# Experts in two passes, with the next feed-forward run on each finished quarter of the width

## The chip, the core and the metric

The kernel runs on one core of a Trainium2 chip. TensorE (PE) multiplies matrices into PSUM, VectorE (DVE) and ScalarE (ACT) do elementwise work, GpSimd (POOL) hardly anything here, SyncE (SP) issues the transfers from device memory. What counts is the device time of one execution in microseconds; before the change it was 1604.07 (median of three, 1603.33 to 1605.59).

## The reference, cut to what matters

Two models stand one behind the other on 256 positions of width 1024. The first block ends with a mixture of 16 experts of which each takes its 32 best positions; the second block (two layers) begins with a feed-forward of width 2816.

```python
# end of the first block
aff = softmax(h @ w_router)                      # h = rms_norm(x)
gate, idx = top_k(aff.T, 32)                     # per expert
xin = h[idx]                                     # (16, 32, 1024)
hid = silu(xin @ w_gate) * (xin @ w_up)          # per expert, 1024 x 1024 each
y = (hid @ w_down) * gate
x = x + zeros.at[idx].add(y)
# start of the second block, layer 0
h = x + 0.5 * (silu(n(x) @ w_gate) * (n(x) @ w_up)) @ w_down   # n = rms_norm, 1024 -> 2816 -> 1024
# then a mixer, a second feed-forward, and the same again for layer 1
```

## The kernel before

Activations are held transposed, 128 channels by 256 positions, eight chunks `xt[:, c]`. All weights come once from device memory as one stream of 1 MB tiles (128 x 2048 words): `add` lists them in order, `fetch` (L308) issues the transfer of the next, `pump` (L316) issues as many as there are slots. A slot is one of 4 "raw" ones or, for expert weights, also one of the 17 of the ring, from which `st["hold"]` keeps some back. The ring also holds activations and the split weights.

The weights of the dense layers are cut into a high and a low part (`split`, `cut`, L325 to L342): ACT writes the high part, DVE the rest, two halves per tile, both into ring slots. A product is then the high part with both parts of the input and the low part with the input's high part. `mm3` (L417) does it as three matmuls of 256 columns into one sum, `mm2` (L422) as one of 512 columns and one of 256, whose two halves are added on the way out of PSUM. One block below is one such product of 128 x 128 weights with 256 positions. Expert weights are used as they are.

Experts (L1200 to L1268), for each of 16 in turn: 8 tiles of gate and up (`gu`, four matmuls per tile in four column groups of the array), Silu and product (`sg`, `hid`), a transposition (`tr`, `hidT`), then 4 tiles of down, one per 256 columns of the width (`y`), each followed by a copy (`ys`) and two matmuls with the matrix `scat` that add the expert's 32 rows at their positions into `macc` (`moe`). The sums of all 16 experts stay in four PSUM banks, and are complete only with the last expert. `keep_warm` puts matmuls without use (`junk`) where PE waits.

The feed-forward (`ffn`, L1273) has 22 gate and up tiles, each one unit of 128 hidden channels (16 blocks), and 11 down tiles. For the first one `first_phase` (L554) starts on the chunks as the last scatters finish. PSUM's eight banks are two pools of four (`pa` and `pb`; `pc` is `pb`), which change roles after each feed-forward (`st["turn"]`).

The order on each engine is set by a scheduler that works with costs of its own and the priorities in the code; `later` and `behind` put something back or in order. So the order of the code isn't that of an engine.

## Time and profile before

| | us |
|---|---|
| median of three runs | 1604.07 |
| the profiled execution | 1605.56 |
| its span, first to last instruction | 1603.8 |
| PE busy in the span | 1478.1 (92%) |
| DVE busy | 892.7 (56%) |
| ACT busy | 666.0 (42%) |
| bytes moved | 400.66 MB, 250 GB/s on the mean |

Matmuls are pipelined and their ends are modelled, so busy PE time says when PE had work and not how fast it went; the distance from start to start says that. The granted clock is a share of 2.4 GHz: 1.00 is that level, 0.50 is 1.2 GHz, and a figure between is a mean over both. A matmul in plain 32-bit floats has two records in the trace, so eight records of `gu` are the four matmuls of one tile.

### The profile page before, as it was taken

The numbers are of one execution on the slowest core, as the hardware profiler recorded it, in microseconds if no ns is written. First come the engines' busy times: TensorE is split into PE (matmuls) and PEld (weight loads), VectorE is DVE, ScalarE is ACT, GpSimd is POOL, SyncE is SP. The second block draws the span as 40 slices with busy tenths as digits, with TensorE's granted clock in tenths as the row PEclk, the third lists the DMA queues.
The fourth block names the chain that finished last, engine by engine and source line by source line (L and its number), as shares of the span: only waits on it lengthen the run. The fifth ranks groups of instructions, "written<-read, shape, count | busy, mean of one in ns | idle before, by whom it ended". The sixth has DMA issues, their size and how long they took to land.

```text
span 1603.8 us, 24974 instructions
## 1 busy us (share of the span) xinstructions
PE 1478.1 (92%) x10328; PEld 1146.4 (71%) x10328; DVE 892.7 (56%) x1680; ACT 666.0 (42%) x1168; POOL 6.1 (0%) x11
## 2 busy tenths in 40 slices
PE   9899988766777768999999999999999999999997
PEld 8887743322223224888889998888888899988886
DVE  7875512100000000977767977766876749877673
ACT  6445211000000000665545665555655546666462
POOL 0000000000000000000000000000000000000000
PEclk9999999877877788999999999999999999999999
DMA  7536799999999999665462545645463643635540
GB/s 295 194 104 226 292 378 420 421 421 421 420 422 421 421 421 410 223 233 207 163 218 94 211 164 192 221 164 210 163 231 135 238 146 126 252 135 211 183 158 27
DMA packets 59153, 400.66 MB, mean 250 GB/s; under 512 B 6560, under 2 KB 9760, under 8 KB 11424
## 3 DMA queue, kind: packets, MB, share of 16 engines
q1 hardware_dynamic: 58896, 398.93, 65.1%
q8 instruction: 81, 1.33, 0.3%
q14 instruction: 32, 0.26, 0.0%
q10 hardware_dynamic: 144, 0.14, 0.0%
HBM read 397.99 MB, written 1.05 MB: 249 GB/s over the span
## 4 chain that ended last, share of the span: by engine, by line
PE 69%; DMA 23%; DVE 5%; ACT 3%; issue 1%; DVEq 0%; SPq 0%; ACTq 0%
DMA w<-in_we 22%; PE gu L425 20%; PE gu L426 10%; PE dn L425 10%; PE dn L426 5%; PE acc L419 1%; PE gu L1217 1%; PE acc L418 1%; PE acc L420 1%; PE y L1260 1%; DVE wl L342 1%; ACT wh L341 1%; PE moe L1245 1%; PE junk L377 1%; PE qk L420 1%
## 5 line engine op out<-in xcount | busy, mean ns | idle before, releaser
L425 PE MATMUL gu<-xs,wh 128*128 128x512 f32 x1408 | 494.7, 395 | 0.0
L342 DVE TENSOR_TENSOR wl<-w,wh 128x1024 fp32r<-128x1024 f32 (+1 forms) x365 | 436.0, 1217 | 39.1 <-ACT wh L341 29.3
L426 PE MATMUL gu<-xs,wl 128*128 128x256 f32 x1408 | 392.0, 279 | 0.0
L341 ACT ACTIVATE wh<-w 128x1024 fp32r<-128x1024 f32 (+1 forms) x365 | 364.0, 1047 | 37.1 <-PE dn L425 20.5
L425 PEld LDWEIGHTS gu<-xs,wh 128*128 128x128 f32 x1408 | 263.7, 188 | 60.7
L426 PEld LDWEIGHTS gu<-xs,wl 128*128 128x128 f32 x1408 | 265.3, 188 | 0.5
L425 PE MATMUL dn<-hx,wh 128*128 128x512 f32 x704 | 248.5, 394 | 0.0
L426 PE MATMUL dn<-hx,wl 128*128 128x256 f32 x704 | 196.2, 279 | 0.0
L1217 PE MATMUL gu<-w,xin 128*32 128x512 f32 x1024 | 139.9, 651 | 45.3 <-DMA w<-in_we 43.9
L425 PEld LDWEIGHTS dn<-hx,wh 128*128 128x128 f32 x704 | 132.0, 187 | 30.8
L426 PEld LDWEIGHTS dn<-hx,wl 128*128 128x128 f32 x704 | 132.6, 188 | 0.0
L1245 PE MATMUL moe<-scat,ys 128*128 128x256 f32 x256 | 92.0, 495 | 28.4 <-DVE ys L1267 15.7
L1267 DVE COPY ys<-y 128x256 f32<-128x256 f32 x34 | 14.4, 424 | 186.4 <-PE y L1260 186.3
L1217 PEld LDWEIGHTS gu<-w,xin 128*32 128x32 f32 x1024 | 26.6, 112 | 127.5 <-DMA w<-in_we 87.9
L1287 ACT ACTIVATE fl<-gu 128x256 f32<-128x256 f32 x176 | 65.9, 377 | 122.5 <-PE gu L426 122.1
L1288 DVE TENSOR_TENSOR fz<-gu,fl 128x256 f32<-128x256 f32 x176 | 73.8, 420 | 71.7 <-ACT fl L1287 71.3
L1233 ACT ACTIVATE sg<-gu 64x512 f32<-64x512 f32 x16 | 9.5, 591 | 249.0 <-PE gu L1217 249.0
L1245 PEld LDWEIGHTS moe<-scat,ys 128*128 128x128 f32 x256 | 54.5, 236 | 73.5 <-DVE ys L1267 33.2
L1234 DVE TENSOR_TENSOR hid<-sg,gu 64x512 f32<-64x512 f32 x16 | 11.0, 690 | 157.0 <-ACT sg L1233 157.0
L1260 PE MATMUL y<-w,hidT 128*32 128x256 f32 x1024 | 91.2, 482 | 7.7 <-ACT hidT L1240 7.7
L1260 PEld LDWEIGHTS y<-w,hidT 128*32 128x32 f32 x1024 | 32.3, 128 | 51.0 <-issue 32.2
L1290 ACT ACTIVATE fs<-fz 128x256 f32<-128x256 f32 x88 | 36.5, 415 | 72.7 <-DVE fz L1289 72.3
(381 smaller groups left out, 2034.2 us busy)
## 6 DMA issues: line engine op xcount, KB each, us to landing
w<-in_we SPq DMA_DIRECT2D x192, 1024.0 KB, 19.8
w<-in_ffn1gu SPq DMA_DIRECT2D x44, 1024.0 KB, 5.0
w<-in_ffn2gu SPq DMA_DIRECT2D x44, 1024.0 KB, 4.9
w<-in_ffn1d SPq DMA_DIRECT2D x22, 1024.0 KB, 5.0
w<-in_wm SPq DMA_DIRECT2D x22, 1024.0 KB, 4.9
w<-in_ffn2d SPq DMA_DIRECT2D x22, 1024.0 KB, 5.0
w<-in_w SPq DMA_DIRECT2D x14, 1024.0 KB, 5.5
w<-in_wo SPq DMA_DIRECT2D x8, 1024.0 KB, 5.0
```

Source lines behind the costliest of these rows:

```text
L341: hi = S.activation(wh, raw[i][:, a0:a1], AF.Copy)
L342: lo = V.tensor_tensor(wl, raw[i][:, a0:a1], wh.bitcast(F32), op=OP.subtract)
L377: PE.matmul(junk[:, :128], lhsT=w, rhs=x, start=True, stop=True)
L420: PE.matmul(ps, lhsT=wh, rhs=x[:, 1], start=False, stop=last, skip_group_check=True)
L425: PE.matmul(ps, lhsT=wh, rhs=x, start=first, stop=False, skip_group_check=True)
L426: PE.matmul(ps[:, 0], lhsT=wl, rhs=x[:, 1], start=False, stop=last, skip_group_check=True)
L1217: PE.matmul(pg[32 * g:32 * g + 32], lhsT=xin[k // 4][:, k % 4, 32 * e:32 * e + 32], rhs=w[:, g], start=k == 0, stop=k == 7, skip_group_che ...
L1245: PE.matmul(macc[s][:, m], lhsT=ys[s][:, 128 * m:128 * m + 128], rhs=sc, start=e == 0 and m == 0, stop=e == NE - 1 and m == 1, skip_group_ ...
L1260: PE.matmul(p[32 * g:32 * g + 32], lhsT=hT[:, g, k // 4], rhs=w[:, k], start=k < 4, stop=k >= 4, skip_group_check=True, tile_position=(0, ...
L1287: S.activation(zl[:, m], p[m][:, 0], AF.Copy)
L1288: V.tensor_tensor(z[:, m], p[m][:, 1], zl[:, m], op=OP.add)
L1290: S.activation(s, z[:, 0], AF.Silu)
```

## The change

The stream and the order of the experts change, and the first feed-forward of layer 0 gets code of its own.

- All 16 experts' gate and up come first (128 tiles). Their hidden values stay in two ring slots (`HT`), the positions' matrices of four experts each in `SC`.
- Down is stored anew: by quarter of the width, then by group of four experts (4 x 4 x 4 tiles). The four matmuls that run side by side in the array's column groups now belong to four experts, a group's sums stand below one another in one bank, and one pair of scatter matmuls serves all four.
- When a quarter (256 channels, two chunks) is complete (`x`), it is added to the residual, multiplied by the norm's weights and split. In the next quarter's 16 tiles the 22 units of the feed-forward's gate and up are computed on these two chunks (`u`): four blocks each, by `mm3`. The partial sums go to six ring slots (`Pt`): copied by ACT for the first quarter, added by DVE for the next ones. Their weights (`f0g`, `f0h`) are stored by quarter, 5.5 MB each, and stand between the down tiles in the stream.
- 5 units of the third quarter (`KEEP`) are kept until after the last down tile. The last quarter of the units runs with `down`, which now covers the full width at once, by `mm3` into four banks; root and Silu come only then.
- The extra `keep_warm` calls in the last expert and `first_phase` go. PSUM's second pool is 3 banks, and `pc` has one of its own.

```diff
@@ -32,7 +32,8 @@
...
 RING, RAW, T1, T2 = 17, 4, 10, 10
-WARM = (12, 32, 8, 3)
+WARM = (12, 32)
+KEEP, EARLY = 5, 2
 ATTN = (1, 1, 1, 1, 2)
...
@@ -158,13 +159,21 @@
...
     g, u = f["w_expert_gate"][0], f["w_expert_up"][0]
     gu = np.concatenate([g.reshape(NE, 8, 128, 1024), u.reshape(NE, 8, 128, 1024)], axis=3)
-    dn = f["w_expert_down"][0].reshape(NE, 8, 128, 4, 256).transpose(0, 3, 2, 1, 4).reshape(NE, 4, 128, 2048)
-    out["we"] = np.concatenate([gu, dn], axis=1)
+    out["we"] = gu
+    dn = f["w_expert_down"][0].reshape(4, 4, 4, 2, 128, 4, 256)
+    out["wd"] = dn.transpose(5, 0, 2, 4, 3, 1, 6).reshape(4, 4, 4, 128, 2048)
...
-        return psum.tile(list(shape), F32, name=name, tag="AB"[st["turn"]], bufs=4)
+        return psum.tile(list(shape), F32, name=name, tag="A", bufs=4)
     def pb(name, shape=(128, 2, 256)):
-        return psum.tile(list(shape), F32, name=name, tag="BA"[st["turn"]], bufs=4)
+        return psum.tile(list(shape), F32, name=name, tag="B", bufs=3)
     def pc(name, shape=(128, 512)):
-        return pb(name, shape)
+        return psum.tile(list(shape), F32, name=name, tag="C", bufs=1)
+    def bank_sets():
+        n = iter(range(1 << 30))
+        def other(name, shape=(128, 2, 256)):
+            return (pb, pb, pb, pc)[next(n) % 4](name, shape)
+        return (other, pa) if st["turn"] else (pa, other)
...
-    WE = [add(a["we"][e], 12, 0) for e in range(NE - 1)]
+    WE = [add(a["we"][e], 8, 0) for e in range(NE)]
...
-    WE.append(add(a["we"][NE - 1], 11, 0))
-    first_gu = add(a["ffn1gu0"], 1, 1)
...
-    def add_ffn(n, l, *gu):
-        gu, dn = list(gu), []
-        for j in range(len(gu), NF):
+    def quarters():
+        for q in range(4):
+            yield from (("y", 0, q, i) for i in range(4))
+            yield ("sc", 0, q)
+        yield ("x", 0)
+        for s in range(1, 4):
+            n, todo = 0, 22 if s < 3 else 22 - KEEP
+            sc = None
+            for k in range(16):
+                yield ("y", s, k // 4, k % 4)
+                while n < todo and n * 13 < (k - 2) * todo:
+                    yield ("u", s - 1, n)
+                    n += 1
+                if sc:
+                    yield sc
+                sc = ("sc", s, k // 4) if k % 4 == 3 else None
+            while n < todo:
+                yield ("u", s - 1, n)
+                n += 1
+            yield sc
+            yield ("x", s)
+        yield from (("u", 2, j) for j in range(22 - KEEP, 22))
+    order, DS, GS = [], {}, {}
+    for op in quarters():
+        if op[0] == "y":
+            order.append(op[1:])
+        elif op[0] == "u" and op[2] % 4 == 0:
+            order.insert(len(order) - EARLY, ("gs", op[1], op[2] // 4))
+    for o in order:
+        if o[0] == "gs":
+            GS[o[1:]], = add([a["f0g"][o[1], o[2]] if o[2] < 5 else a["f0h"][o[1]]], 1, 1)
+        else:
+            DS[o], = add([a["wd"][o]], 1, 0)
+    d0 = []
+    for j in range(22):
...
-    macc = [pa(f"moe{b}") for b in range(4)]
...
-        sd = work.tile([128, 2, 4, 32], F32, name="sgr", tag="t1", bufs=T1)
-        for t in range(2):
-            V.tensor_scalar(sd[:, t], onehot[t][:, e].bitcast(F32)[:, None, :].to_broadcast([128, 4, 32]),
-                            aff[:, t, e:e + 1], None, op0=OP.mult)
-        pt = pc("tr")
-        for t in range(2):
-            PE.transpose(pt[:, 256 + 128 * t:384 + 128 * t], sd[:, t].rearrange("p g s -> p (g s)"), ident)
-        sc = t1("scat")
-        V.tensor_copy(sc, pt[:, 256:512])
         sg = work.tile([64, 512], F32, name="sg", tag="t2", bufs=T2)
         hid = work.tile([64, 512], F32, name="hid", tag="t2", bufs=T2)
         S.activation(sg, pg[0:64], AF.Silu)
...
-        hT = work.tile([128, 4, 2, 32], F32, name="hidT", tag="t1", bufs=T1)
-        S.activation(hT.rearrange("p j h s -> p (j h s)"), pt[:, 0:256], AF.Copy)
-        py, ys = [pb("y0", (128, 512)), pb("y1", (128, 512))], {}
-        def scatter(s):
+        if e % 8 == 0:
+            HT.append(ralloc([128, 8, 2, 4, 32], F32, "hidT"))
+            st["hold"] -= 1
+        S.activation(HT[e // 8][:, e % 8].rearrange("p h j s -> p j h s"),
+                     pt[:, 0:256].rearrange("p (j h s) -> p j h s", j=4, h=2), AF.Copy)
+        if e % 4 == 3:
+            q = e // 4
+            ps = pa("trs")
+            for t in range(2):
+                sd = work.tile([128, 4, 32], F32, name="sgr", tag="t1", bufs=T1)
+                V.tensor_tensor(sd, onehot[t][:, 4 * q:4 * q + 4].bitcast(F32),
+                                aff[:, t, 4 * q:4 * q + 4, None].to_broadcast([128, 4, 32]), op=OP.mult)
+                PE.transpose(ps[:, 0, 128 * t:128 * t + 128], sd.rearrange("p g s -> p (g s)"), ident)
+            if q % 2 == 0:
+                SC.append(t2("scat"))
+            V.tensor_copy(SC[q // 2][:, q % 2], ps[:, 0])
...
+    def quarter_steps():
+        norm, Pt, py, ys, macc = None, [], {}, {}, {}
+        def unit(s, j):
+            i = GS[s, j // 4]
+            n = 4 if j < 20 else 2
+            ahead(i)
+            wh, wl = (w[:, :512 * n].rearrange("p (c j m o) -> p c j m o", c=2, j=n, m=2) for w in parts[i])
+            p = pb("gu")
             for m in range(2):
-                PE.matmul(macc[s][:, m], lhsT=ys[s][:, 128 * m:128 * m + 128], rhs=sc,
-                          start=e == 0 and m == 0, stop=e == NE - 1 and m == 1, skip_group_check=True)
-        for s in range(4):
-            pump()
-            if e == NE - 1 and s == 3:
-                f = GU["ffn1", 0]
-                norm, ps0 = Norm(vc("ffn1n", 0, 8)), [pb("gu"), pb("gu")]
-                front = first_phase(norm, adder(macc), f[0], ps0, lambda c: c == 5 and split(f[1]))
...
-            p = py[s // 2][:, 256 * (s % 2):256 * (s % 2) + 256]
-            for k in range(8):
-                g = k % 4
-                PE.matmul(p[32 * g:32 * g + 32], lhsT=hT[:, g, k // 4], rhs=w[:, k],
-                          start=k < 4, stop=k >= 4, skip_group_check=True, tile_position=(0, 32 * g))
...
-            ys[s] = t1("ys")
-            if s % 2 or e == NE - 1:
-                st["ys"] = V.tensor_copy(ys[s], p)
+                for c in range(2):
+                    mm3(p[:, m], wh[:, c, j % 4, m], wl[:, c, j % 4, m], norm.x[2 * s + c], m == 0 and c == 0,
+                        m == 1 and c == 1)
+            if j % 4 == n - 1:
+                done(i)
+            return p
+        for op in quarters():
+            if op[0] == "y":
+                _, s, q, i = op
+                pump()
+                if i == 0:
+                    py[s, q] = pa("y", (128, 256))
+                k = DS[s, q, i]
+                w = raw[k].rearrange("p (k g n) -> p k g n", k=2, g=4)
+                for c in range(2):
+                    for g in range(4):
+                        e = 4 * q + g
+                        h = HT[e // 8][:, e % 8].rearrange("p h j s -> p (h j) s")
+                        PE.matmul(py[s, q][32 * g:32 * g + 32], lhsT=h[:, 2 * i + c], rhs=w[:, c, g],
+                                  start=i == 0 and c == 0, stop=i == 3 and c == 1, skip_group_check=True,
+                                  tile_position=(0, 32 * g))
+                done(k)
+                if i == 3:
+                    ys[s, q] = t1("ys")
+                    S.activation(ys[s, q], py.pop((s, q)), AF.Copy)
+            elif op[0] == "sc":
+                _, s, q = op
+                if q == 0:
+                    macc[s] = pa("moe")
+                y = ys.pop((s, q))
+                for m in range(2):
+                    PE.matmul(macc[s][:, m], lhsT=y[:, 128 * m:128 * m + 128], rhs=SC[q // 2][:, q % 2],
+                              start=q == 0 and m == 0, stop=q == 3 and m == 1, skip_group_check=True)
+            elif op[0] == "x":
+                s = op[1]
+                if norm is None:
+                    norm = Norm(vc("ffn1n", 0, 8))
+                for m in range(2):
+                    c = 2 * s + m
+                    V.tensor_tensor(xt[:, c], macc[s][:, m], xt[:, c], op=OP.add)
+                    norm.split(c)
+                for m in range(2):
+                    norm.square(2 * s + m)
+                if s == 0:
+                    st["hold"], st["la"], st["late"] = 7, 1, 0
+                if s == 3:
+                    rfree(2)
             else:
-                S.activation(ys[s], p, AF.Copy)
-            scatter(s)
-            if e == NE - 1 and s == 3:
-                next(front)
-    rfree(2)
...
+                _, s, j = op
+                p = unit(s, j)
+                if s == 0:
+                    if j % 4 == 0:
+                        Pt.append(ralloc([128, 4, 2, 256], F32, "Pt"))
+                        st["hold"] -= 1
+                    S.activation(Pt[j // 4][:, j % 4], p, AF.Copy)
+                else:
+                    V.tensor_tensor(Pt[j // 4][:, j % 4], p, Pt[j // 4][:, j % 4], op=OP.add)
+        return norm, Pt, unit
...
+    def first_ffn():
+        st["hold"] = 5
+        norm, Pt, unit = quarter_steps()
+        warm(AF.Silu)
+        st["hold"], st["la"], st["late"] = 1, LA[0], LATE[0]
+        ps, hs, acc = {}, {}, []
+        def evac(j):
+            z = Pt[j // 4][:, j % 4]
+            V.tensor_tensor(z, ps.pop(j), z, op=OP.add)
+            V.tensor_tensor(z, z, norm.rb2, op=OP.mult)
+            s, h = t1("fs"), t1("fh")
+            S.activation(s, z[:, 0], AF.Silu)
+            V.tensor_tensor(h, s, z[:, 1], op=OP.mult)
+            hs[j] = t2("hx", F32R)
+            hilo(hs[j][:, 1], hs[j][:, 0], h)
+        def down(j):
+            if j == 0:
+                acc.extend(pa(f"dn{b}") for b in range(4))
+            i = d0[j // 2]
+            ahead(i)
+            wh, wl = (w.rearrange("p (m o j) -> p m o j", m=2, j=128) for w in parts[i])
+            for o in range(8):
+                mm3(acc[o // 2][:, o % 2], wh[:, j % 2, o], wl[:, j % 2, o], hs[j], j == 0 and o % 2 == 0,
+                    j == NF - 1 and o % 2 == 1)
+            if j % 2:
+                done(i)
+        for j in range(3):
+            ps[j] = unit(3, j)
+            if j == 0:
+                norm.fin1(pa)
+        norm.fin2()
+        for j in range(3):
+            evac(j)
+        for j in range(3, NF):
+            ps[j] = unit(3, j)
+            evac(j)
+            down(j - 3)
+        norm.free()
+        st["hold"], st["la"], st["late"] = 2, LA[1], LATE[1]
+        for j in range(NF - 3, NF):
+            down(j)
+        rfree(6)
+        return adder(acc, 0.5)
+    def ffn(update, n, l, g):
+        P, Q = bank_sets()
         gu, dn = GU[n, l], DN[n, l]
...
```

What stands where is told by the order of each engine's instructions.

PE at an expert, kernel before. In the names, `w183` to `w187` are tiles of the stream, `hidT` the expert's hidden values.

```order
L1217 MATMUL gu_4044<-w182_3924,xin1_2369 32x512 x4
L1217 MATMUL gu_4044<-w183_3930,xin1_2369 32x512 x4
L1238 MATMUL tr_4094<-cst_86,hid_4100 128x64 x4
L1260 MATMUL y0_4109<-w184_3936,hidT_4107 32x256 x8
L1245 MATMUL moe0_2324<-scat_4097,ys_4121 128x256 x2
L1260 MATMUL y0_4109<-w185_3942,hidT_4107 32x256 x8
L1245 MATMUL moe1_2325<-scat_4097,ys_4135 128x256 x2
L1260 MATMUL y1_4110<-w186_3948,hidT_4107 32x256 x8
L1245 MATMUL moe2_2326<-scat_4097,ys_4149 128x256 x2
L1260 MATMUL y1_4110<-w187_3954,hidT_4107 32x256 x8
L1245 MATMUL moe3_2327<-scat_4097,ys_4163 128x256 x2
```

PE in the fourth quarter's down, kernel after. `w216` to `w220` are down tiles of four experts each, `gu` the units of the third quarter, `xs` the normed input.

```order
L1296 MATMUL y_4750<-w216_4690,hidT_2423 32x256 x8
L1296 MATMUL y_4750<-w217_4700,hidT_2423 32x256 x8
L1309 MATMUL moe_4773<-scat_2653,ys_4854 128x256 x2
L1296 MATMUL y_4872<-w219_4720,hidT_2957 32x256 x8
L1296 MATMUL y_4872<-w220_4798,hidT_2957 32x256 x5
L479 MATMUL gu_4818<-xs_3551,wl214_4811 128x256
L480 MATMUL gu_4818<-xs_3551,wh214_4810 128x256
L481 MATMUL gu_4818<-xs_3551,wh214_4810 128x256
```

Scatters went from one pair behind each tile to one pair behind each four; 48 matmuls of four units follow here, before the last 3 of tile `w220`.

SP at the end of the experts, kernel before: the issues in order.

```order
L313 DMA w_4167<-in_we 128x2048
L313 DMA w_4174<-in_we 128x2048
L313 DMA w_4180<-in_we 128x2048
L313 DMA w_4186<-in_we 128x2048
L313 DMA w_4192<-in_we 128x2048
L313 DMA w_4198<-in_we 128x2048
L313 DMA w_4289<-in_ffn1gu 128x2048
```

SP in the fourth quarter's down, kernel after.

```order
L374 DMA w_4686<-in_f0g 128x2048
L374 DMA w_4688<-in_wd 128x2048
L374 DMA w_4690<-in_wd 128x2048
L374 DMA w_4700<-in_wd 128x2048
L374 DMA w_4718<-in_f0g 128x2048
L374 DMA w_4720<-in_wd 128x2048
L374 DMA w_4798<-in_wd 128x2048
L374 DMA w_4800<-in_wd 128x2048
L374 DMA w_4816<-in_f0g 128x2048
```

The feed-forward's tiles have moved from behind the experts to every third or fourth place among the down tiles.

DVE in the first feed-forward, kernel before: `fz` are sums out of PSUM, `wl` low parts of weights, `fh` and `hx` the hidden values.

```order
L1288 TENSOR_TENSOR fz<-gu,fl 128x256 x2
L1289 TENSOR_TENSOR fz<-fz,rb 128x512
L1291 TENSOR_TENSOR fh<-fs,fz 128x256
L455 TENSOR_TENSOR hx<-fh,hx 128x256
L342 TENSOR_TENSOR wl_5611<-w_5428,wh_5610 128x1024 x2
```

DVE in the feed-forward's last quarter, kernel after: `Pt` are the partial sums.

```order
L1350 TENSOR_TENSOR fh<-fs,Pt 128x256
L403 TENSOR_TENSOR wl_5431<-w_5234,wh_5430 128x1024 x2
L516 TENSOR_TENSOR hx<-fh,hx 128x256
L403 TENSOR_TENSOR wl_5531<-w_5236,wh_5530 128x1024
L1346 TENSOR_TENSOR Pt<-gu,Pt 128x512
L403 TENSOR_TENSOR wl_5531<-w_5236,wh_5530 128x1024
L1347 TENSOR_TENSOR Pt<-Pt,rb 128x512
L403 TENSOR_TENSOR wl_5561<-w_5238,wh_5560 128x1024 x2
```

Two additions of 256 columns became one of 512, and the splits of gate, up and down tiles stand closer together.

## Rows read from the trace of the kernel before

**Rows 1.** The page, part 2: the span in 40 slices of 40.1 us.

```profile
PE   9899988766777768999999999999999999999997
...
PEclk9999999877877788999999999999999999999999
...
GB/s 295 194 104 226 292 378 420 421 421 421 420 422 421 421 421 410 223 233 207 163 218 94 211 164 192 221 164 210 163 231 135 238 146 126 252 135 211 183 158 27
```

**Rows 2.** Busy time by stage (us, each engine's busy us, granted clock, DMA).

```profile
core 0: us, PE busy (x) PEld busy (x) DVE busy (x) ACT busy (x) POOL busy (x), PEclk, DMA share, GB/s
...
191.00:200.00 9.00, 6.50 (x35) 3.62 (x34) 6.03 (x14) 0.69 (x1) 0.00 (x0) 0.83 0.01 4
200.00:216.00 16.00, 13.94 (x87) 6.39 (x86) 4.03 (x6) 3.94 (x5) 0.00 (x0) 0.99 0.87 311
216.00:640.00 424.00, 322.91 (x2341) 125.66 (x2341) 40.14 (x124) 29.42 (x65) 0.00 (x0) 0.82 1.01 420
...
650.00:833.00 183.00, 183.00 (x1057) 159.83 (x1056) 138.65 (x217) 104.05 (x175) 0.00 (x0) 1.00 0.61 216
```

**Rows 3.** The chain of waits (start us, us, what).

```profile
349.85 19.81 DMA w<-in_we
369.72 19.82 DMA w<-in_we
...
602.46 21.29 DMA w<-in_we
623.78 1.94 PE gu L1217 x8
```

**Rows 4.** Timeline of SP at the end of the experts (start us, us, instruction).

```profile
623.80 0.33 SPq L313 DMA_DIRECT2D w<-in_we  x1
```

**Rows 5.** Timeline of PE in the first feed-forward.

```profile
700.13 0.39 PE L425 MATMUL gu<-xs,wh 128*128 128x512 f32 x1
700.36 0.27 PE L426 MATMUL gu<-xs,wl 128*128 128x256 f32 x1
700.47 0.40 PE L425 MATMUL gu<-xs,wh 128*128 128x512 f32 x1
...
700.82 0.39 PE L425 MATMUL dn<-hx,wh 128*128 128x512 f32 x1
```

**Rows 6.** Timeline of two experts, all engines.

```profile
370.49 1.07 PE L1260 MATMUL y<-w,hidT 128*32 128x256 f32 x16
...
372.12 1.13 PE L1245 MATMUL moe<-scat,ys 128*128 128x256 f32 x4 [0.56 <-ACT ys L1269]
...
375.92 1.06 PE L1217 MATMUL gu<-w,xin 128*32 128x512 f32 x8
...
384.62 1.89 PE L1217 MATMUL gu<-w,xin 128*32 128x512 f32 x8 [1.43 <-DMA w<-in_we]
...
389.58 1.07 PE L1217 MATMUL gu<-w,xin 128*32 128x512 f32 x8 [0.93 <-DMA w<-in_we]
390.71 0.59 ACT L1233 ACTIVATE sg<-gu 64x512 f32<-64x512 f32 x1 [18.65 <-PE gu L1217]
...
393.29 1.93 PE L1260 MATMUL y<-w,hidT 128*32 128x256 f32 x16 [0.52 <-ACT hidT L1240]
```

**Rows 7.** Timeline of PE in the mixer's first projection.

```profile
836.09 0.28 PE L418 MATMUL lx<-xs,wl 128*128 128x256 f32 x1
836.21 0.28 PE L419 MATMUL lx<-xs,wh 128*128 128x256 f32 x1
836.33 0.28 PE L420 MATMUL lx<-xs,wh 128*128 128x256 f32 x1
836.45 0.28 PE L418 MATMUL lx<-xs,wl 128*128 128x256 f32 x1
```

**Rows 8.** Instruction groups of 640 to 860 us (busy us, mean ns, idle before).

```profile
L342 DVE TENSOR_TENSOR wl<-w,wh 128x1024 fp32r<-128x1024 f32 x78 | 93.4, 1219 | 6.6 <-ACT wh L341 4.3 <-PE gu L425 1.8 <-issue 0.2
...
L1287 ACT ACTIVATE fl<-gu 128x256 f32<-128x256 f32 x44 | 16.4, 375 | 27.5 <-PE gu L426 27.4
L1289 DVE TENSOR_TENSOR fz<-fz,rb 128x512 f32<-128x512 f32 x22 | 15.1, 687 | 0.2
...
L1291 DVE TENSOR_TENSOR fh<-fs,fz 128x256 f32<-128x256 f32 x22 | 9.3, 421 | 4.8 <-ACT fs L1290 4.8
L455 DVE TENSOR_TENSOR hx<-fh,hx 128x256 fp32r<-128x256 f32 x22 | 9.1, 423 | 5.4 <-ACT hx L454 5.0
...
L1385 DVE TENSOR_TENSOR L<-lx,rb 128x512 f32<-128x512 f32 x1 | 0.7, 683 | 0.0
```

129 lines of the change are left out of this document (45 added, 84 removed).

## The prediction

> **What bounds the kernel now.** The page's 40 slices come first [rows 1]. DMA moves 420 to 422 GB/s in slices 7 to 15 and half of that or less later; TensorE (PE) is below nine tenths busy in just these slices, and its granted clock is 7 or 8 tenths there. So there are two regimes: experts bound by DMA, then a second block bound by PE with DMA half idle. The table by stage [rows 2] sets the borders: 216 to 640 us at 420 GB/s, PE busy 323 of 424 us at a mean granted clock of 0.82; then the first feed-forward from 650 to 833 us, PE busy 183.0 of 183 us at 1.00 and DMA at 216 GB/s. The chain of waits agrees: through the experts its links are the landing of expert weights, 19.8 us each with eight in flight [rows 3], until PE takes over at 623.8. One 1 MB tile therefore costs 19.81 / 8 = 2.48 us; 1.0486 MB at 421 GB/s gives 2.49, which I use.
>
> The last expert tile is issued at 623.80 [rows 4] and, at the usual 19.8 us, lands at 643.6. Nothing of the first feed-forward (352 + 176 weight blocks) can run before, since it needs the experts' sum. One block (two matmuls, 512 and 256 columns) takes 0.345 us, from starts at 700.13 and 700.82 two apart [rows 5]; 528 x 0.345 = 182 us, which is the stretch 650 to 833.
>
> **What the change does to the bound.** A quarter of the width of the experts' sum is complete after 16 down tiles, so the feed-forward's gate and up can start on it while the other quarters still come in. PE work that DMA now makes wait is to be filled in, at the price of more bytes ahead of the last expert tile.
>
> **DMA, up to the last down tile.** Before: 128 gate and up tiles, 64 down, 1 of the feed-forward = 193. After: 128 + 64 + three quarters' worth of feed-forward gate and up, 3 x 5.5 = 208.5. That is 15.5 x 2.49 = 38.6 us more: 643.6 becomes 682 if DMA never stands still. The hold of the ring is 2 or 1 where it was 0 at the start of the experts, so two tiles fewer are ahead when DMA restarts (it stood at 4 GB/s from 191 to 200 and ran at 311 until 216 [rows 2]). Bounds: 0, and 2 x 2.49 = 5 us. I take 3, as PE no longer stops for the first expert's down: 685.
>
> **PE in that stretch.** Gate and up: 8 matmul records per tile, 1.06 us at the higher clock and 1.89 at the lower [rows 6], both under 2.49, so the first 128 tiles stay bound by DMA. Then, per quarter, 16 down tiles at 1.07 us (16 records, higher clock) = 17.1; four scatters at 1.13 = 4.5 [rows 6] (16 in all where there were 64, since one now serves four experts); and, from the second quarter on, 22 units of four blocks on the quarter before. A block is now three matmuls of 256 columns. The mixer has this form: 0.36 us from 836.09 to 836.45 [rows 7]. So 22 x 4 x 0.36 = 31.7, and a full quarter is 53.3 us of PE against 21.5 x 2.49 = 53.5 of DMA. The third round has 17 units, 46.1. The two are equal, so neither can catch up when it has waited for the other. That is the weak point. While a quarter fills, ring slots go to the 6 tiles of partial sums, 2 of normed input, 2 of hidden values, 1 of the residual and 2 to 4 of split weights; by the program's counts the stream keeps 4 raw slots and one to three of the ring. PE's order has runs of 48 to 72 unit matmuls without a down tile, 5.8 to 8.6 us, in which DMA fills 2.3 to 3.5 tiles; and runs of four or five down tiles at 2.49 us with 1.07 us of work. The first round also begins cold, since down tiles alone leave PE 57% idle.
>
> What DMA stands still in all: from below 0; from above, if half of the units' time in the three quarters lay beside no transfer, 3 x 16 = 48 us. I take 12: the buffers hold about five tiles, and PE falls behind by some 8 us of clustered units a quarter for two quarters plus a few us of lower clock, of which five tiles (12.5 us) cover half, while the third round, 7 us shorter on PE, takes back the rest. The third quarter of the feed-forward's input is then done at 697.
>
> **Splits.** ScalarE and VectorE (DVE) do the same 16.5 MB of splits in the three quarters, 2 x 1.219 us per tile on DVE [rows 8], 13.4 a quarter, with 22 additions at 0.69 (683 ns from PSUM, 687 ns from SBUF, both 128x512 [rows 8]) 28.6 of 53: hidden. The copies of the first round on ScalarE show no row of 128x512 from PSUM; nearest below is 64x512 at 0.59 us [rows 6], above, twice 375 ns [rows 8]: 13 to 17 us a quarter, hidden as well, since they stand after the splits.
>
> **After the last down tile.** The last tile, its copy and scatter: 1 us. The five units kept back (7.2 us) hide the addition, norm and split of the last two chunks. Then the last quarter with all of down: 22 x (4 + 8) x 0.36 = 95.0 us of PE. DVE there: 16.5 tiles x 2.44 = 40.2, plus 22 x (0.69 + 0.69 + 0.42 + 0.42) = 48.8, together 89 of 95 us [rows 8]. Before, DVE was busy 138.7 of 183 [rows 2]. Where this cover is thin, waits between ScalarE and DVE show: bounds 0, and 22 x 0.69 = 15 us (one exposed 128x512 operation per unit); I take 4. The first down waits for the reciprocal root, its turn, the multiplication, Silu, a product and a split in two: six dependent operations of about 0.4 to 0.7 us, 3.5 us, of which two to three units cover part; with the small ones of the root, 4 us, bounds 0 and 8.
>
> Sum: 685 + 12 + 1 + 7.2 + 95.0 + 4 + 4 = 808, where the mixer began at 833. Minus 25 us. The profiled run took 1605.56 with a span of 1603.8; 1605.6 - 25 = 1580.6, and as that run stood 1.5 us above the median, 1579.
>
> In sentences that the sum does not need: the Trainium skill, page "TensorE: Matmul & The Clock Gate", section "Back-to-back issue gap", gives N / 2.4 + 2.5 ns for a warm matmul, so 327 ns for three of 256 columns and 325 for 512 plus 256. The trace has 360 and 345 [rows 5, 7], so the form with three matmuls does cost; by the page the last quarter would be 8.6 us shorter (an estimate from that page) and the sum 1570.
>
> **Removed or moved at nothing.** The extra warming matmuls at the last expert stand in PE's waits for DMA. In the first block PSUM's second pool is 3 banks and 1 apart instead of 4 together, which moves projections ahead of the recurrence; the matmul count to the router is the same 1405. It costs 0, with 3 us either way, paid in full since the first expert matmul waits for it. The last 4662 matmuls stand in the old order: 0, with 2 either way.
>
> **Rivals.**
> Steady DMA: the slots suffice, nothing stands still and the two waits of 4 us do not show: 685 + 103 = 788, minus 45: 1559. For it: 420 GB/s through 424 us [rows 2]. Against: there, 16 tiles could be ahead, here five.
>
> Cold PE: the granted clock in the quarters stays at the experts' 0.82 [rows 2] instead of 1.00. Each of two full rounds takes 53.3 / 0.82 = 65 us, the third 56; 186 for 160.5, so 26 us of lost time where I took 12, and some 3 us in the last units: 1596. For it: in the expert stage the same work takes 1.06, 1.89, 1.07 and (down) 1.93 us within 18 us [rows 6], so half full stretches do fall to the lower level of 1.2 GHz. Against: wherever PE is dense, the clock is 1.00 [rows 2]. The Trainium skill, same page, section "HAM oscillation", says that a PE which waits for DMA between short bursts starts each burst at half clock, and asks for dense work; this stage has both patterns, so it bears on the chance alone.
>
> Slower, taking turns: a split tile or a down tile behind a run of units holds the slot that the next transfer needs, and so on round the four raw slots, so that transfers and units alternate. At half of the units' time exposed in the three rounds, and the last quarter DVE-bound with 15 instead of 4: 48 + 15 - 16 = 47 us over the forecast, less what the third round gives back (7): 1619. It decides from 25 us over my two figures of 12 and 4. For it: equal demands and few slots. Against: splits stand ahead of the additions on DVE, so tiles leave early.
>
> No effect: the order rows show that units do stand between down tiles, so this has little.
>
> **Chances.** Forecast 0.46 (1568 to 1590), steady DMA 0.22 (1553 to 1568), cold PE 0.18 (1588 to 1603), turns 0.12 (1607 to 1630), none 0.02. Within 0.2% (1601 to 1607) is about what a measurement cannot tell from no change. Faster: 0.46 + 0.22 + 0.15 = 0.83; same 0.05; slower 0.12. Range for 8 in 10: 1556 to 1606.
>
> **What would show it.** Right: about 420 GB/s into the 680s, the last down tile between 682 and 705, PE busy 9 tenths or more at a clock near 1 from the second quarter on, the mixer's first matmul at 800 to 815, an unchanged time from there to the end. Steps wrong: DMA gaps in the quarters with PE busy (standstill too small), DMA full and PE waiting (term too large), matmuls of 256 columns at lower clock there (cold PE), PE waiting for DVE in the last quarter above 4 us, or a first expert matmul not near 197. The prediction fails if the last down tile lands after 720, or the last quarter takes over 115 us.

## The result, and the profile after

The changed kernel takes 1581.62 us (median of four, 1579.60 to 1582.37); the kernel before, in the same rounds, 1604.83. The ratio is 0.9852, 95% interval 0.9835 to 0.9869: 23 us less, where 25 were forecast. The profiled execution took 1579.6 with a span of 1577.8.

The page of the changed kernel, its 40 slices of 39.4 us, against [rows 1]:

```profile
PE   9999986676666789899999999999999999999997
...
PEclk9999997766768899999999999999999999999998
...
GB/s 297 195 131 225 307 393 421 421 421 421 421 421 421 360 344 351 402 354 184 232 128 163 241 119 220 179 191 156 217 184 187 224 117 173 242 117 221 170 161 27
```

The plateau of 421 GB/s now ends with slice 13; slices 14 to 18 are the quarters, at 344 to 402. The table by stage, with the columns of [rows 2], shows the same in us:

```profile
200.00:500.00 300.00, 206.28 (x1245) 41.82 (x1243) 18.44 (x55) 21.14 (x40) 0.00 (x0) 0.74 1.01 418
500.00:540.00 40.00, 25.85 (x225) 14.89 (x221) 4.40 (x7) 7.14 (x14) 0.00 (x0) 0.79 0.98 407
540.00:580.00 40.00, 38.41 (x372) 29.89 (x372) 10.83 (x10) 17.73 (x27) 0.00 (x0) 1.00 0.89 346
580.00:620.00 40.00, 34.25 (x317) 25.71 (x316) 16.36 (x23) 12.25 (x18) 0.00 (x0) 0.91 0.85 338
620.00:660.00 40.00, 33.75 (x340) 24.24 (x338) 18.65 (x26) 7.61 (x13) 0.00 (x0) 1.00 0.94 368
660.00:700.00 40.00, 37.36 (x342) 29.69 (x342) 19.28 (x23) 9.56 (x12) 0.00 (x0) 0.96 0.98 385
700.00:780.00 80.00, 80.00 (x677) 78.43 (x676) 77.79 (x126) 49.55 (x76) 0.00 (x0) 1.00 0.65 228
```

Standstill of DMA is read from the last column: a row of 40 us at 346 GB/s has lost 40 x (1 - 346/421) = 7.1. The rows from 500 to 700 give 1.3 + 7.1 + 7.9 + 5.0 + 3.4 = 24.8 us, where 12 were forecast. PE is idle beside it for 30 of the 200 us: each waits for the other in turn. From 700 on PE is full at clock 1.00.

The last down tile and the mixer's `qk`, in PE's timeline and by tile (count, ns min/median/max, first and last start):

```profile
702.38 1.07 PE L1296 MATMUL y<-w,hidT 128*32 128x256 f32 x16
```

```profile
L479 PE MATMUL qk<-xs,wl x64: 278/283/363, 808.5 to 840.7; 128*128 128x256 f32 x64
```

In the kernel before, the same matmuls of `qk` began at 834.7:

```profile
L418 PE MATMUL qk<-xs,wl x64: 277/283/365, 834.7 to 866.9; 128*128 128x256 f32 x64
```

26 us are gained by then, and from there to the end of the span it takes 769.1 us before and 769.3 after. The mixer's first matmuls, of `lx`, stand 0.7 us before these: at 807.8, and at 833.9 before. (These are the two profiled executions; between the medians it is 23 us.)

The start of the experts moved too. By tile, the first gate and up matmuls of the changed kernel:

```profile
L1233 PE MATMUL gu<-w,xin x1024: 592/617/1064, 190.6 to 470.9; 128*32 128x512 f32 x171
```

the first eight of them in PE's timeline,

```profile
190.62 1.07 PE L1233 MATMUL gu<-w,xin 128*32 128x512 f32 x8
```

and the same place in PE's timeline of the kernel before:

```profile
197.07 1.94 PE L1217 MATMUL gu<-w,xin 128*32 128x512 f32 x8 [0.78 <-ACT xin L1157]
```

The experts begin 6.5 us earlier, and not at the lower clock (592 to 617 ns a record, 1.07 us for eight, where the eight of the kernel before took 1062 each, 1.94 in all). The cause lies in the first block, from 40 to 80 us, the changed kernel first, the kernel before second:

```profile
40.00:80.00 40.00, 39.72 (x836) 35.91 (x835) 37.55 (x50) 16.50 (x22) 0.00 (x0) 1.00 0.54 191
```

```profile
40.00:80.00 40.00, 35.68 (x670) 32.00 (x669) 35.85 (x48) 16.23 (x20) 0.00 (x0) 0.91 0.53 195
```

With the other PSUM pools PE has 4 us less idle time there, a granted clock of 1.00 instead of 0.91, and does 166 records more. Nearly all of that idle time is one wait of the kernel before for VectorE in the recurrence:

```profile
57.81 1.08 PE L804 MATMUL lev<-AR,AL 128*32 128x32 f32 x64 [3.88 <-DVE AL L849]
```

### The profile page after: what moved, and what is told of

Read it like the earlier page. It is cut to its first block, busy times and chain, and to the rows that moved or that the text cites. A ratio compares the mean times of both kernels' runs of the same rounds, so it can differ in the third digit from the quotient of the medians.

```text
span 1577.8 us, 25243 instructions
## 1 busy us (share of the span) xinstructions
PE 1436.9 (91%) x10552; PEld 1121.4 (71%) x10552; DVE 890.6 (56%) x1628; ACT 660.1 (42%) x1136; POOL 6.1 (0%) x11
## 4 chain that ended last, share of the span: by engine, by line
PE 69%; DMA 23%; DVE 5%; ACT 2%; issue 1%; SPq 0%; DVEq 0%; ACTq 0%
DMA w<-in_we 16%; PE gu L486 16%; PE gu L487 8%; PE dn L486 8%; DMA w<-in_wd 6%; PE dn L487 4%; PE gu L479 3%; PE gu L480 2%; PE gu L481 2%; PE y L1296 2%; PE acc L480 2%; PE acc L479 1%; PE acc L481 1%; DVE wl L403 1%; PE dn L479 1%; PE dn L481 1%
## 5 line engine op out<-in xcount | busy, mean ns | idle before, releaser
L486 PE MATMUL gu<-xs,wh 128*128 128x512 f32 x1056 | 371.7, 395 | 0.0
L1233 PE MATMUL gu<-w,xin 128*32 128x512 f32 x1024 | 182.3, 806 | 67.8 <-DMA w<-in_we 67.5
L486 PEld LDWEIGHTS gu<-xs,wh 128*128 128x128 f32 x1056 | 197.9, 188 | 45.9
L486 PE MATMUL dn<-hx,wh 128*128 128x512 f32 x528 | 186.6, 394 | 0.0
L487 PE MATMUL dn<-hx,wl 128*128 128x256 f32 x528 | 147.5, 279 | 0.0
L486 PEld LDWEIGHTS dn<-hx,wh 128*128 128x128 f32 x528 | 99.0, 187 | 23.2
L481 PE MATMUL gu<-xs,wh 128*128 128x256 f32 x352 | 100.7, 287 | 0.0
L480 PE MATMUL gu<-xs,wh 128*128 128x256 f32 x352 | 100.7, 287 | 0.0
L487 PEld LDWEIGHTS dn<-hx,wl 128*128 128x128 f32 x528 | 99.6, 189 | 0.0
L1394 ACT ACTIVATE fl<-gu 128x256 f32<-128x256 f32 x132 | 49.4, 377 | 95.7 <-PE gu L487 95.4
L1395 DVE TENSOR_TENSOR fz<-gu,fl 128x256 f32<-128x256 f32 x132 | 55.2, 419 | 57.3 <-ACT fl L1394 57.1
```

The lines of the kernel that those rows point to most:

```text
L480: PE.matmul(ps, lhsT=wh, rhs=x[:, 0], start=False, stop=False, skip_group_check=True)
L481: PE.matmul(ps, lhsT=wh, rhs=x[:, 1], start=False, stop=last, skip_group_check=True)
L486: PE.matmul(ps, lhsT=wh, rhs=x, start=first, stop=False, skip_group_check=True)
L487: PE.matmul(ps[:, 0], lhsT=wl, rhs=x[:, 1], start=False, stop=last, skip_group_check=True)
L1233: PE.matmul(pg[32 * g:32 * g + 32], lhsT=xin[k // 4][:, k % 4, 32 * e:32 * e + 32], rhs=w[:, g], start=k == 0, stop=k == 7, skip_group_che ...
L1394: S.activation(zl[:, m], p[m][:, 0], AF.Copy)
```

## The experiments

Each is an edit of the changed kernel unless it says otherwise, and `...` marks what is left out of an edit. three_slots, one_matmul, no_sums and one_turn_low leave out or overwrite part of the sums, so their output isn't the reference's. Standstill and PE's idle time are those from 500 to 660 us, where the quarters of all kernels but units_behind and before_pools are still running, worked out from the table by stage as above.

| kernel | us | ratio to before (95%) | DMA stands | PE idle |
|---|---|---|---|---|
| changed kernel | 1581.62 | 0.9852 (0.9835 to 0.9869) | 21.3 | 27.7 |
| units_behind | 1603.16 | 0.9986 (0.9976 to 0.9996) | | |
| before_pools | 1595.61 | 0.9933 (0.9913 to 0.9953) | | |
| three_slots | 1584.54 | 0.9867 (0.9848 to 0.9886) | 20.3 | 22.6 |
| one_matmul | 1568.23 | 0.9760 (0.9738 to 0.9783) | 12.5 | 43.6 |
| pool_low | 1576.52 | 0.9818 (0.9802 to 0.9834) | 19.4 | 27.2 |
| no_sums | 1578.52 | 0.9833 (0.9818 to 0.9847) | 18.7 | 27.3 |
| pe_in_turn | 1572.62 | 0.9796 (0.9781 to 0.9811) | 16.5 | 23.2 |
| even | 1590.64 | 0.9913 (0.9896 to 0.9930) | 31.1 | 28.9 |
| turn_low | 1564.24 | 0.9743 (0.9722 to 0.9763) | 8.4 | 18.7 |
| one_turn_low | 1555.28 | 0.9691 (0.9674 to 0.9707) | 1.1 | 41.7 |
| even_low | 1553.87 | 0.9683 (0.9666 to 0.9699) | 2.3 | 9.5 |
| even_pool | 1615.14 | 1.0066 (1.0047 to 1.0085) | 47.1 | 42.1 |

**units_behind: the same kernel without units between the down tiles.**

```diff
-KEEP, EARLY = 5, 2
+KEEP, EARLY = 5, 0
...
-            n, todo = 0, 22 if s < 3 else 22 - KEEP
...
-                while n < todo and n * 13 < (k - 2) * todo:
-                    yield ("u", s - 1, n)
-                    n += 1
...
-            while n < todo:
...
-        yield from (("u", 2, j) for j in range(22 - KEEP, 22))
+        for s in range(3):
+            yield from (("u", s, j) for j in range(22))
```

> This kernel takes the experts and down by quarters as the changed kernel does, but computes the units of the first three quarters only after the last down tile, with their weights behind it in the stream. Theory (the gain is the units' time beside the transfers of down): up to the last down tile there are 16.5 tiles less and no standstill, so it is used at about 703.5 - 41 - 25 = 637 us; then some 4 us for the last chunks, 66 units x 1.44 = 95 us and the last quarter as before, so the mixer begins at about 831 to 835 instead of 808: 1604 to 1610 us, the gain gone. Rival (the gain comes from the order of the experts and the 48 pairs of scatters saved, 54 us of TensorE): 1582 to 1590.

1603.16, just under the theory's range. Two passes with the new PSUM pools and no units between gain next to nothing; the units on finished quarters are worth 1603.2 - 1581.6 = 21.5 us. (The change as a whole is worth less than that, since without the units the two passes stand behind the next kernel, which has the pools alone.)

**before_pools: the kernel before with the new PSUM pools.** From the experts on the pools' roles are swapped in the code, so that the order stays that of the kernel before; of the edit only the pools themselves are shown.

```diff
-        return psum.tile(list(shape), F32, name=name, tag="AB"[st["turn"]], bufs=4)
+        return psum.tile(list(shape), F32, name=name, tag="A", bufs=4)
...
-        return psum.tile(list(shape), F32, name=name, tag="BA"[st["turn"]], bufs=4)
+        return psum.tile(list(shape), F32, name=name, tag="B", bufs=3)
...
-        return pb(name, shape)
+        return psum.tile(list(shape), F32, name=name, tag="C", bufs=1)
...
```

> The kernel before, with the PSUM pools of the changed one (4, 3 and 1 banks; roles swapped from the experts to the first feed-forward so that the rest keeps its order). Up to the router TensorE's order is that of the changed kernel, from the experts on that of the kernel before. Theory (the 6.6 us by which the changed kernel reaches the router earlier, 171.9 against 178.5, are the pools' doing and pass whole into the end, since the DMA-bound stage restarts with the first expert matmul): router at about 172, 1597 to 1600 us, ratio 0.996. Rival (the early start is lost in the DMA-bound stage, which has its own restart): router at 172, but 1603 to 1606.

1595.61: the early start is not lost, it grows. SP's timeline at the end of its experts, and its mixer:

```profile
612.18 0.33 SPq L322 DMA_DIRECT2D w<-in_we  x1
```

```profile
L427 PE MATMUL qk<-xs,wl x64: 278/283/365, 824.6 to 856.8; 128*128 128x256 f32 x64
```

The last expert tile is issued 11.6 us earlier than in [rows 4] and `qk` begins 10.1 earlier. That is the 6.5 of the first block, and a DMA that is back at full rate sooner: between 200 and 220 us it moves 422 GB/s, where the kernel before moves 331 and the changed kernel, with slots held back, 375. So up to 10 of the 26 us have nothing to do with the experts' order. Against this kernel the changed one is 1595.6 - 1581.6 = 14.0 us faster, and units_behind 7.6 slower: the two passes cost time of their own, which the units then more than win back. What of that cost is the held ring, the block of three matmuls or the order was not tried apart. (Nor was the changed kernel with the first block in its old order.)

**three_slots: three ring slots more for the stream.** The partial sums take three tiles instead of six.

```diff
-                    st["hold"], st["la"], st["late"] = 7, 1, 0
+                    st["hold"], st["la"], st["late"] = 4, 1, 0
...
-                        Pt.append(ralloc([128, 4, 2, 256], F32, "Pt"))
-                        st["hold"] -= 1
+                        if j < 12:
+                            Pt.append(ralloc([128, 4, 2, 256], F32, "Pt"))
+                            st["hold"] -= 1
+                        else:
+                            Pt.append(Pt[j // 4 - 3])
...
```

> The changed kernel with the partial sums in 3 ring slots instead of 6: units j and j + 12 share one place, so the feed-forward's output isn't the reference's; all work is still done. Three more slots hold the stream. Theory (DMA's 25 us of standstill in the quarters come from too few slots): DMA above 395 GB/s on the mean of 520 to 680, standstill 10 us or less, 1564 to 1573 us. Rival (equal demand and the fixed order of instructions make the waits, slots or not): GB/s as in the changed kernel, 1578 to 1583.

1584.54, not faster. The theory with which I began, too few slots, fell.

**one_matmul: a block of the first three quarters is one matmul.**

```diff
+                    if s < 3:
+                        PE.matmul(p[:, m], lhsT=wl[:, c, j % 4, m], rhs=norm.x[2 * s + c][:, 1],
+                                  start=m == 0 and c == 0, stop=m == 1 and c == 1, skip_group_check=True)
+                        continue
```

> The changed kernel with one matmul instead of three in each block of the first three quarters' units (the products with the weights' high part are left out, so the output isn't the reference's); transfers, splits and additions stay. A full quarter needs 32 us of TensorE instead of 53. Theory (DMA stands still because runs of units keep TensorE from the down tiles that hold the slots): the quarters are bound by DMA at 410 GB/s or more, the last down tile is used at 679 to 684 instead of 703.5, and with kept units of 2.4 instead of 7.2 us, of which some 3 us come back as the last chunks' latency, 1552 to 1561 us. Rival (the splits or SyncE's queue hold the slots): GB/s of 340 to 400 in the quarters as now, 1570 or more.

1568.23, between the two. PE is idle for 43.6 of 160 us, and DMA still stands for 12.5: PE's demand is a part, and something holds slots that is not the amount of PE's work.

What that can be, the timelines of DVE and ACT in the changed kernel show (start, us, in brackets the idle time before and who ended it):

```profile
601.90 0.69 DVE L1334 TENSOR_TENSOR Pt<-gu,Pt 128x512 f32<-128x512 f32 x1 [7.02 <-PE gu L481]
...
610.99 0.69 DVE L1334 TENSOR_TENSOR Pt<-gu,Pt 128x512 f32<-128x512 f32 x1 [1.93 <-PE gu L481]
611.60 1.22 DVE L403 TENSOR_TENSOR wl<-w,wh 128x1024 fp32r<-128x1024 f32 x1
```

```profile
599.60 2.01 ACT L402 ACTIVATE wh<-w 128x1024 fp32r<-128x1024 f32 x2 [6.17 <-PE y L1296]
612.02 0.39 ACT L1302 ACTIVATE ys<-y 128x256 f32<-128x256 f32 x1 [10.41 <-PE y L1296]
612.30 1.05 ACT L402 ACTIVATE wh<-w 128x1024 fp32r<-128x1024 f32 x1
```

The high half is there at 600.7. Its low half begins at 611.6, behind seven additions of which each waits for a unit; the next high half stands right behind a copy that waits for a down tile. Until the low half is written the raw tile keeps its slot. So a new theory, late splits, with two parts to be told from it: runs of up to six units between two down tiles on PE, and equal demands.

**pool_low: no split stands behind a copy or an addition that waits for PE.** (The set of tiles `LOW` is that of the first three quarters.)

```diff
+    LOW = set(GS.values())
...
-        lo = V.tensor_tensor(wl, raw[i][:, a0:a1], wh.bitcast(F32), op=OP.subtract)
+        lo = (G if i in LOW else V).tensor_tensor(wl, raw[i][:, a0:a1], wh.bitcast(F32), op=OP.subtract)
...
-                    ys[s, q] = t1("ys")
-                    S.activation(ys[s, q], py.pop((s, q)), AF.Copy)
+                    V.tensor_copy(ys[s, q], py.pop((s, q)))
...
-                    S.activation(Pt[j // 4][:, j % 4], p, AF.Copy)
+                    V.tensor_copy(Pt[j // 4][:, j % 4], p)
```

> The low halves of the split of the feed-forward's gate and up tiles of the first three quarters are computed on GpSimd instead of DVE, and the copies of the partial sums and of the experts' output move from ScalarE to DVE, so that no split stands behind an operation that waits for PE. The trace of the changed kernel shows high halves 6 to 13 us after the tile's landing, behind such copies on ScalarE, and low halves behind runs of up to seven additions on DVE (one at 611.6 whose high half began at 599.6); the tile's slot is held all that time, and DMA stands still for 24.8 us between 500 and 700 us. Theory (splits late in their engines' order): the standstill falls to 10 us or less and the time to 1562 to 1570. Rival (runs of several units between down tiles on PE set when slots come free): 1578 to 1585. If a low half of 128x1024 takes GpSimd more than 4 us, which no row shows yet, its queue becomes the bound and the time is above 1585.

1576.52: 5 us, between both ranges, the interval just clear of the changed kernel's; the standstill is only 2 us shorter. ACT's waits from 515 to 700 us (line, total us, times, longest) say that its high halves still waited for PE more than for their tile:

```profile
ACT wh L403 <- PE gu L482: 53.9, 6, 11.2
ACT wh L403 <- DMA w<-in_f0g: 20.3, 5, 5.5
```

They are written to ring slots which, by the program, come free with the units of an earlier tile. More slots for split weights were not tried.

**no_sums: no copies and additions of partial sums.**

```diff
+                        G.memset(Pt[-1].rearrange("p j m t -> p (j m t)"), 0.0)
...
-                    S.activation(Pt[j // 4][:, j % 4], p, AF.Copy)
-                else:
-                    V.tensor_tensor(Pt[j // 4][:, j % 4], p, Pt[j // 4][:, j % 4], op=OP.add)
```

> The copies and additions of the partial sums in the first three quarters are left out (the sums' tiles are filled with zeros once by GpSimd, so that their slots are still taken; the output then lacks three quarters of the gate's and up's input). ScalarE keeps the splits, ten copies of the experts' output and the normed input; DVE the splits and the normed input. Theory (late splits): the low halves start at once, high halves can only stand behind the copies of the experts' output; standstill 10 to 15 us, 1567 to 1573. Rival (runs of units on PE): PE's matmuls are the same, so 1578 to 1584.

1578.52, in the rival's range, and its interval overlaps the changed kernel's.

**pe_in_turn: PE's order tied to the program's.** The first matmul of each unit is put behind the last of the down tile before it, and the reverse.

```diff
+                    if s < 3 and m + c == 0:
+                        behind(first, last[0])
+            if s < 3:
+                last[:] = [end]
...
+                        if last and c + g == 0:
+                            behind(mm, last[0])
+                last[:] = [mm]
```

> PE's order in the three quarters is tied to the order in which the program is written: one or two units after each down tile (2.9 us of PE at most) instead of runs of up to six units (8.6 us) and pairs of down tiles. DVE and ScalarE get almost the order they had. Theory (late splits): the splits stand where they stood, 1576 to 1584. Rival (runs of units on PE): down slots come free every 2.5 to 4 us, the standstill of 24.8 us falls to 10 or less and the time to 1563 to 1571.

1572.62: 9 us, again between the ranges. Runs of units cost time, and are not all.

**even: as pe_in_turn, the units spread over all 48 down tiles.**

```diff
+        n = 0
...
-            n, todo = 0, 22 if s < 3 else 22 - KEEP
...
-                while n < todo and n * 13 < (k - 2) * todo:
-                    yield ("u", s - 1, n)
+                while n < 66 - KEEP and n * 16 < (16 * s + k - 18) * 22:
+                    yield ("u", n // 22, n % 22)
...
-            while n < todo:
...
```

> As pe_in_turn, and the units are spread evenly: 22 units to 16 down tiles throughout, so that a quarter's last four or five units run beside the next quarter's first down tiles (the first unit still waits for the first quarter's end). In pe_in_turn DMA stood still for 19.6 us between 500 and 700 us and PE was idle for 25.1: PE waits for transfers while three down tiles pass without a unit, and then transfers wait for PE. Theory (the two demands are equal over a quarter but not within it): three tiles without units leave PE idle for 3 x (2.49 - 1.07) = 4.3 us in each of the two later quarters, which comes back as standstill; without it 1563 to 1568. Rival (late splits alone are left): 1570 to 1574.

1590.64, 18 us slower than pe_in_turn: both expectations were wrong in sign. SP's waits from 500 to 700 us (line, total us, times, longest):

```profile
SPq L371 <- PE y L1297: 93.2, 29, 6.2
SPq L371 <- DVE wl L400: 62.8, 15, 13.1
```

In the changed kernel the second of these is `33.3, 14, 7.0`. Spread out, the four units of one tile end later, and the next split stands behind their copies, as in ACT's timeline:

```profile
554.36 0.60 ACT L1336 ACTIVATE Pt<-gu 128x512 f32<-128x512 f32 x1 [2.03 <-PE gu L478]
554.85 1.99 ACT L399 ACTIVATE wh<-w 128x1024 fp32r<-128x1024 f32 x2
```

From the first to the fifth tile of the first quarter the high halves begin 14.2 us apart on the mean (526.07 to 582.75), in pe_in_turn 10.7 (526.53 to 569.13).

**turn_low: pe_in_turn and pool_low together** (both diffs).

> pe_in_turn and pool_low together: PE's units in turn with the down tiles, and low halves on GpSimd, copies and additions on DVE, high halves alone on ScalarE. Theory (late splits cost time beside what PE's order costs): 4 to 5 us less than pe_in_turn's 1572.6, as pool_low gained 5 on the changed kernel: 1566 to 1569. Rival (with PE in turn, splits are no longer late enough to count): 1571 to 1574.

1564.24, 8.4 us under pe_in_turn, more than expected: 9.0 and 5.1 alone, 17.4 together. The 3.3 us over the sum are not clear of noise: the kernel before, run beside these kernels, had medians of 1603.9 to 1605.9.

**one_turn_low: turn_low with one_matmul's blocks** (all three diffs).

> As turn_low, and every block of the units of the first three quarters is one matmul instead of three (the two larger products are left out), so that PE's demand per quarter falls from 53 to about 32 us. Theory (runs of units on PE, late splits and equal demands are all there is): DMA stands still for less than 6 us between 500 and 690, 1554 to 1561. Rival (a fourth cause: slots or the order of the DMA queue itself): 12 us or more of standstill are left, as in one_matmul (19.2), and 1565 to 1569.

1555.28, as the theory has it. Next to nothing, 1.1 us, is left of the standstill up to 660:

```profile
540.00:580.00 40.00, 28.27 (x276) 16.42 (x280) 13.89 (x25) 8.68 (x12) 17.78 (x9) 0.91 1.01 419
...
620.00:660.00 40.00, 29.62 (x264) 16.95 (x260) 13.12 (x23) 8.43 (x11) 14.02 (x6) 0.83 1.01 421
```

So with less work on PE neither the slots nor the order of the DMA queue show as a fourth cause.

**even_low: even and pool_low together.**

> As turn_low, with the units spread evenly as in even. Theory (all three causes): the gains add up, 1559 to 1565, the fastest of these kernels that computes everything. Rival (one cause covers the others): 1566 to 1572.

1553.87, faster than expected and than every other kernel here, 28 us under the changed kernel and 50 under the one before. Spreading the units, which cost 18 us on pe_in_turn, gains 10 on turn_low. Its stages, and ACT's timeline:

```profile
540.00:580.00 40.00, 40.00 (x408) 30.84 (x400) 14.84 (x26) 8.70 (x12) 19.39 (x10) 1.00 1.01 414
580.00:620.00 40.00, 40.00 (x396) 31.15 (x389) 12.43 (x20) 8.03 (x8) 18.96 (x8) 1.00 1.01 419
620.00:660.00 40.00, 39.51 (x394) 30.02 (x394) 14.64 (x25) 10.04 (x14) 17.14 (x9) 1.00 1.00 407
```

```profile
536.78 2.01 ACT L400 ACTIVATE wh<-w 128x1024 fp32r<-128x1024 f32 x2 [7.98 <-issue]
546.78 2.01 ACT L400 ACTIVATE wh<-w 128x1024 fp32r<-128x1024 f32 x2 [7.99 <-DMA w<-in_f0g]
556.78 2.01 ACT L400 ACTIVATE wh<-w 128x1024 fp32r<-128x1024 f32 x2 [7.98 <-DMA w<-in_f0g]
```

DMA and PE are both full. In these rows a gate and up tile is split every 10.0 us, and what ended the wait is its landing where the row names anything; with its 2.9 down tiles that is 3.9 tiles, 9.7 us of DMA.

**even_pool: even_low with the copies back on ScalarE.**

```diff
-                    V.tensor_copy(ys[s, q], py.pop((s, q)))
+                    S.activation(ys[s, q], py.pop((s, q)), AF.Copy)
...
-                    V.tensor_copy(Pt[j // 4][:, j % 4], p)
+                    S.activation(Pt[j // 4][:, j % 4], p, AF.Copy)
```

> even_low did two things to the splits at once: the low halves went to GpSimd, and the copies went from ScalarE to DVE. Here only the low halves go to GpSimd; the copies of the partial sums and of the experts' output stay on ScalarE, ahead of high halves. Theory (a split is late by whichever engine's order it stands in): high halves still wait behind copies, so the time lies between even_low's 1553.9 and even's 1590.6, at 1562 to 1578. Rival (only the low halves behind DVE's additions counted): 1552 to 1557.

1615.14, slower than the kernel before, beyond either range. ACT's timeline:

```profile
544.52 0.60 ACT L1337 ACTIVATE Pt<-gu 128x512 f32<-128x512 f32 x1 [2.90 <-PE gu L479]
545.01 1.99 ACT L400 ACTIVATE wh<-w 128x1024 fp32r<-128x1024 f32 x2
553.17 0.60 ACT L1337 ACTIVATE Pt<-gu 128x512 f32<-128x512 f32 x1 [6.16 <-PE gu L479]
...
562.39 0.60 ACT L1337 ACTIVATE Pt<-gu 128x512 f32<-128x512 f32 x1 [2.03 <-PE gu L479]
562.89 1.99 ACT L400 ACTIVATE wh<-w 128x1024 fp32r<-128x1024 f32 x2
```

This shows the loop. A tile's high halves (545.01) are followed by its low halves, two of 2.3 us on GpSimd; then its four units with their down tiles pass on PE, and their copies on ACT; and the next tile's high halves (562.89) stand behind the copy of the last of these units (562.39). The loop takes 17.9 us here, 17.4 on the mean of the quarter's tiles (527.00 to 596.59), where DMA needs 9.7. The two copies alone, on ScalarE or on DVE, make the 61 us between this kernel and even_low. The rival "taking turns" of the prediction has the form of this loop; its 1619 was worked out another way, from half of the units' time. Against even only the low halves moved, to the slower GpSimd, and the time rose by 24.5 us. In the changed kernel the high halves of the same quarter begin at 526.42, 539.73, 545.41, 556.24 and 567.85: 10.4 us apart on the mean, up to 13.3, close to what DMA needs.

## Why the prediction was right, and where it was not

The direction and the mechanism were right: units between the down tiles (21.5 us by units_behind) make the gain of the new order, which is 14.0 us against before_pools. Last down tile at 702 to 703 (682 to 705 named), the mixer's first matmul at 807.8 (sum 808, 800 to 815 named), the rest unchanged. But three terms were off, and that they cancel is luck.

- **"Removed or moved at nothing", first block 0, 3 either way: failed.** It is worth 10 us by before_pools, 6.5 of them before the first expert, whose first matmul came at 190.6, not near 197. The count of matmuls (1405 in both) on which the 0 rested says nothing of PE's waits between them. The hold of the ring at the start, 3 us, was about right: from 180 to 220 us the changed kernel's DMA loses some 3 us more than that of before_pools. Both together: up to 240 us the changed kernel has moved 260 GB/s on the mean and the kernel before 248, which is 2.9 MB or 6.9 us ahead.
- **Standstill 12: it was 24.8, and some 2 from 200 to 500** (418 for 421 GB/s). It stayed inside the bounds, 0 to 48. What failed is that five tiles of buffers cover half of PE's runs and that the third round takes back the rest: three more slots left 20.3 of the 21.3 us up to 660 (three_slots), and from 660 to 700 us, in the third round, another 3.4 were lost. The argument against taking turns, "splits stand ahead of the additions on DVE, so tiles leave early", failed too: low halves stood behind up to seven of them, and high halves behind the copies on ACT, set down as "hidden as well, since they stand after the splits". Two parts, runs of units and equal demands, were named; pe_in_turn shows the runs at 9 us, pool_low the late splits at 5. The sign of 420 GB/s into the 680s failed with it.
- **After the last down tile 111: it was 105,** from 702.4 to 807.8. 1 + 7.2 + 95.0 is 103; the two waits of 4 us hardly showed. DVE was busy 77.79 of 80 us and PE 80.00, so the cover was thin and held. The size of a block was right: 677 records in those 80 us are 118 ns each, 355 for three. The Trainium skill, page "TensorE: Matmul & The Clock Gate", section "Back-to-back issue gap", calls N / 2.4 + 2.5, from which the prediction had 327, the gap of an isolated matmul and gives other spacings for a stream with weight loads; so 327 was not the page's figure for this stretch, and the trace has 355.

Together: -10 + 13 + 2 - 6, about nothing, so the sum of 808 met 807.8 by luck, with wrong parts.

**Cold PE** did not decide: the granted clock of the rows is 0.79 up to 540, while the second quarter starts, and 0.91 to 1.00 from there. **Steady DMA** (1559) did not come about, with 24.8 us of standstill, and its reason, that the slots suffice, was not the one that counts: even_low comes near its condition, with 2.3 us left up to 660, once units and down tiles take even turns and no split stands behind a copy or an addition. PE busy nine tenths from the second quarter on held only in part: 0.96, 0.86, 0.84, 0.93 in the four rows.

What stays open: how the 24.8 us divide by cause within the changed kernel. pool_low gains 5 us, pe_in_turn 9, and leaving out the sums (no_sums) 3 at most; none of these three shortens the standstill by more than 5.

## What to carry to other kernels

An operation that frees a transfer's slot should stand, on its engine, ahead of whatever waits for the work that this transfer feeds; that its engine is half idle says nothing (in even_pool ACT was busy 40 of the 160 us up to 660). Look for the loop (tile lands, is split, used, result copied, next tile split on the same engine), add up its time and compare it with what DMA needs for the tiles of one turn. Evening out the bottleneck engine's work came last here, and before the loop was open it lengthened it and cost time.

## What the runs showed of the hardware that I had not expected

GpSimd, idle before, did the low halves at about half DVE's speed. That moving them there paid is not shown: the fast kernels moved the copies as well, with the copies left on ScalarE it cost 24.5 us (even_pool against even), and the copies on DVE with the low halves left there were not tried. The groups of even_low from 540 to 690 us, GpSimd and then DVE (line, operation, count, busy us, mean ns, idle before):

```profile
L401 POOL TENSOR_TENSOR wl<-w,wh 128x1024 fp32r<-128x1024 f32 x26 | 61.6, 2390 | 59.2 <-ACT wh L400 59.2
```

```profile
L1339 DVE TENSOR_TENSOR Pt<-gu,Pt 128x512 f32<-128x512 f32 x44 | 30.3, 690 | 60.4 <-PE gu L479 60.3
```

The same half takes DVE 1219 ns [rows 8], a ratio of 1.96. That is the ratio which the Trainium skill, page "GPSIMD Engine Reference", section "Elementwise — side-by-side cycle accounting", gives for an addition of two tensors; the trace agrees. DVE's additions, with one input in PSUM, kept their 690 ns (692 in the changed kernel) while GpSimd was busy 69 of these 150 us, so no slowing of them showed.
